# A hybrid decoder layer on one core: value projection of two head pairs in one product of 256 columns

## The chip, the core and the metric

The kernel runs on one NeuronCore of a Trainium2 chip. Its engines are TensorE (PE in the profile; PEld is its weight load), VectorE (DVE), ScalarE (ACT), GpSimd (POOL) and SyncE (SP). POOL, SP and ACT also issue DMAs, each in the order of its own instruction list. The metric is the device time of one execution in microseconds, the median of three runs. The traces come from one further execution under the hardware profiler.

## What is computed

One decoder layer on 2048 tokens of width 1024, in float32. A pre-normalised input `h` goes through one combined projection; eight heads of causal attention with a forget gate ("FoX", branch A) and eight query heads of sliding-window attention with sinks (branch B, two key/value heads) follow; each branch output is multiplied by a SiLU gate, both are concatenated, projected, normalised and added to the residual.

```python
h = rms_norm(x, g_pre[l]) * (1.0 + scale[:, None, :]) + shift[:, None, :]
proj = h @ w_in[l]
qa, ka, va, fa, za, qb, kb, vb, zb = jnp.split(proj, split_points, axis=-1)
oa = forgetting_attention(qa.reshape(B, S, FOX_HEADS, HEAD_DIM),
                          ka.reshape(B, S, FOX_HEADS, HEAD_DIM),
                          va.reshape(B, S, FOX_HEADS, HEAD_DIM), fa + b_fgate[l])
oa = oa * jax.nn.silu(za)
...
ob = sliding_window_sink_attention(qb, kb, vb.reshape(B, S, SWA_KV_HEADS, HEAD_DIM), sinks[l])
ob = ob * jax.nn.silu(zb)
y = jnp.concatenate([oa, ob], axis=-1) @ w_out[l]
x = x + gate[:, None, :] * rms_norm(y, g_post[l])
```

The change is about `va`, the values of branch A: 2048 tokens by 8 heads of 64.

## The kernel before

*Numbers.* Every float32 operand of a projection is split into a high and a low float16 part, and a product is made of three: high x high, low x high and high x low. `hT[ci]` holds the normalised input of 512 tokens (chunk `ci`, four of them), transposed: 128 features on the partitions, 8 groups of features (`k`), 512 tokens. The weights come in keys of 128 columns: `kb`, `vb`, `qb0` to `qb3` and `zb0` to `zb3` for branch B; `va0` to `va3`, `qk0` to `qk7` and `za0` to `za3` for branch A. `va0` is the value weight of heads 0 and 1, and so on in pairs of heads.

*The chain of a key's weights.* Eight steps: `w_load` (L210: one DMA of 512 KB on POOL's queue into a raw tile), `w_max` (L219: maximum per partition on DVE, then a DMA of 128 numbers to DRAM, `mx_d`, on POOL), `w_back` (L227: a DMA that reads the 128 numbers back to every partition, `mxr`, on POOL), `w_scale` (L232: a power of two from them, five small DVE instructions), `w_high` (L250: the high part, one ACT instruction), `w_low` twice (L258: the low part, two DVE instructions), `w_done` (L292: small constants). The raw tiles of all keys rotate through two buffers; the split tiles "whl" of the `va`, `zb` and `za` keys through two others.

*The products.* `proj_units` (L323) gives a projection with the weights stationary: eight units of three products of 512 columns. `value_units` (L339) keeps the tokens stationary, because attention needs the values with tokens on the partitions: for a key and a chunk eight units of 12 products of 128 columns, which fill one PSUM bank with four tiles of 128 tokens by 128 columns. After the last unit ACT copies the bank as float16 to the high half of `vt`, DVE writes the low half in two instructions, and the bank is free again. Three banks, `bk`, serve all projections of this part; `bank(True)` takes one and `release` gives it back. The inner lines:

```python
for k in range(4 * (n_ % 2), 4 * (n_ % 2) + 4):
    for n, (a, b) in enumerate(((0, 0), (1, 0), (0, 1))):
        PE.matmul(ps[:, u * P:(u + 1) * P], hT[ci][:, a, k, u * P:(u + 1) * P], whl[:, b, k, :],
                  start=(k == 0 and n == 0), stop=(k == KT - 1 and n == 2))
```

*The order.* It is written out by hand. `add` (L938) appends units to one list, `punits`, and puts the eight steps of a key's weights as events at positions ahead of its first unit: the load 42 positions ahead, the maximum 31, the read-back 21, the scale 12, the high part 9, the low parts 7 and 5, the constants 4. `fill` (L1081) walks through the list: at each position it issues the events and then the unit. A position is called a slice below. The other work is put around it with lags: `after(n, f)` runs `f` at the n-th `tick` from now.

The first 140 slices are the prologue and run alone, with a tick every second slice. Then come 32 windows of branch B (`Pair`, L852; loop at L1117). In each of them the scores (`pss`, PE), their maxima (DVE, L883), the exponentials (ACT, L894), the transposes (`pxb`, PE), the split of the transposed probabilities (`ptb`: high half on ACT, low half on DVE, L908) and the product with the values (`pob`, PE, L922) are spread over some seven or eight slices, and POOL copies the sinks (L881). The evacuation of a `zb` projection is a tanh on ACT (L376), a multiplication on DVE (L372, tile `tz`) and a DMA to DRAM on POOL (`z_d`). After the windows branch A follows, with more projections between its steps, and the output projection, whose weights and scratch go through a pool of four buffers of 2 KB per partition, `stpo` (L1375).

The projections that follow `kb`, `vb` and `zb0` stand in this order: `zb0`, `zb1`, `va0`, `zb2`, `zb3`, `va1`, `va2` in `others` (L960), mixed with `qb0` to `qb3`; then `va3` for chunks 0 and 1, `qk0`, and `va3` for chunks 2 and 3. The first unit of `va0` is slice 200; `va3` begins at slice 440.

Of the kernel before, what the change touches and what calls it, by code (L numbers as in the profile page):

```python
# [10 lines left out]
F32 = mybir.dt.float32  # L11
F16 = mybir.dt.float16
# [29 lines left out]
def hybrid_layer(  # L42
# [207 lines left out]
    def w_high(key):  # L250
        raw, pw, sw = wq[key]
        width = VB if key == "vb" else P
        pool = vbw if key == "vb" else wpq if key[0] in "qk" else wpool
        whl = pool.tile([P, 2, KT, width], F16, tag="whl", name=f"wh_{key}")
        A.activation(whl[:, 0], raw[:], AF.Identity, scale=sw[:])
        wq[key].append(whl)

# [13 lines left out]
    def o_store(on, pool, ci, rows_, cols_, eng, lag):  # L271
# [11 lines left out]
        after(lag, lambda: A.activation(oh[:, :, 0], on, AF.Copy))  # L283
        after(lag + 1, low)

    pws = {}
    scl, isc, czs, kaps = {}, {}, {}, {}

# [47 lines left out]

        return [lambda k=k: unit(k) for k in range(KT)]

    def value_units(key, ci, dst):  # L339

        st_ = {}

        def unit(n_):
            if n_ == 0:
                st_[0] = bank(True)
            whl, ps = wq[key], bk[st_[0]][:]
            u = n_ // 2
            for k in range(4 * (n_ % 2), 4 * (n_ % 2) + 4):
                for n, (a, b) in enumerate(((0, 0), (1, 0), (0, 1))):
                    PE.matmul(ps[:, u * P:(u + 1) * P], hT[ci][:, a, k, u * P:(u + 1) * P], whl[:, b, k, :],  # L350
                              start=(k == 0 and n == 0), stop=(k == KT - 1 and n == 2))
            if n_ == 7:
                hi, lo = dst()
                pv4 = ps.rearrange("p (t h d) -> p t h d", t=4, h=2)
                after(1, lambda: A.activation(hi, pv4, AF.Copy, scale=PS_SCALE))

                def low():
                    for h in range(2):
                        V.scalar_tensor_tensor(lo[:, :, h], pv4[:, :, h], PS_SCALE, hi[:, :, h],
                                               op0=ALU.mult, op1=ALU.subtract)  # L360
                    release(st_[0])

                after(2, low)

        return [lambda n=n: unit(n) for n in range(8)]

    def evac_z(kt, key, ci):
        def evac(ps, free):
# [304 lines left out]
    def open_fox():  # L673
        nonlocal abp
        xlx.close()
        abp = swa_pool("abp", 4)
        early.close()
        fxv = right.enter_context(tc.tile_pool(name="fxv", bufs=1, side="right", reuse_waits="tile"))
        vt = fx["vt"] = fxv.tile([P, NB, 8, VW], F16, name="vt")
        fx["lk"] = fxv.tile([P, LW], F16, name="lk")  # L680
# [14 lines left out]
    def va_units(j, ci):  # L695
        rows_ = slice(4 * ci, 4 * ci + 4)
        heads = slice(2 * j, 2 * j + 2)
        return value_units(f"va{j}", ci, lambda: (fx["vt"][:, rows_, heads, 0:64], fx["vt"][:, rows_, heads, 65:VW]))


    swa = ExitStack()

# [257 lines left out]
    for kind, j in (("zb", 0), ("zb", 1), ("va", 0), ("zb", 2), ("zb", 3), ("va", 1), ("va", 2)):  # L960
        key = f"{kind}{j}"
        others += [(key, va_units(j, ci) if kind == "va" else proj_units(key, ci, evac_z(4 + j, key, ci)))
                   for ci in range(NCH)]

    def at_slice(n, f):
        events.setdefault(n, []).append(f)
# [54 lines left out]
        n_o = lim  # L1021
    N_SWA = len(punits)
    at_slice(N_SWA - 40, const_turn)
    for ci in range(2):
        add("va3", va_units(3, ci))

    def evac_qk(hd, ci):
        cols_ = slice(ci * CH, (ci + 1) * CH)
# [26 lines left out]
    for ci in range(NCH):  # L1055
        add("qk0", qk_units(0, ci))
    N_QK0 = len(punits)
    for ci in range(2, NCH):
        add("va3", va_units(3, ci))
    N_V3 = len(punits)  # L1060
    for hd in range(1, 7):
        for part in range(6):
# [306 lines left out]
    def open_out():  # L1369
        nonlocal op_, stp  # L1370
        foxl.close()
        hpx.close()
        wo = foxo.enter_context(tc.tile_pool(name="wo", bufs=1, reuse_waits="tile"))
        op_ = foxo.enter_context(tc.tile_pool(name="opo", bufs=2, reuse_waits="tile"))
        stp = foxo.enter_context(tc.tile_pool(name="stpo", bufs=4, reuse_waits="tile"))  # L1375
        oio["w"] = wo.tile([P, 2, KT, D], F16, name="wohl")

        fm = sm(1, "w_p2")
        V.tensor_reduce(fm[:], fac8[:], axis=AX.X, op=ALU.max)
        V.reciprocal(fm[:], fm[:])  # L1380
        V.tensor_tensor(ysc[:], wrt[:], fm[:], op=ALU.mult)
        V.tensor_scalar(wsc[:], fac8[:], ysc[:], None, op0=ALU.mult)
# [19 lines left out]
        V.scalar_tensor_tensor(w_slot(8 + k)[:, cc], raw[:], wsc[:, k:k + 1], hi, op0=ALU.mult, op1=ALU.subtract)  # L1402

    oio = {}

    class Out:

# [315 lines left out]
```

## Time and profile before

| what | value |
|---|---|
| median of three runs | 1190.55 us (1188.28 to 1191.04) |
| the profiled execution | 1184.12 us, its span 1182.4 us |
| granted TensorE clock | 0.993 on average |
| value products (L350) | 1536 products of 128 columns, PE busy 91.0 us |
| their evacuation | 16 on ACT, 596 ns each; 32 on DVE, 416 ns each |
| a load of value weights | 4, landing 5.2 us after issue |

How to read the lines below: the page gives busy time, share of the span and count per engine, then groups of instructions as "line engine operation out<-in xcount | busy us, mean ns of one | idle time before them and what ended it". Matmuls are pipelined and their ends are modelled, so that the busy time or the mean of a product isn't what it costs; the distance from start to start is. The chain of waits follows the work that ended last backwards, and its pieces are lengths from start to start. In the timelines a bracket holds the idle time of the engine just before the instruction, and whom it waited for.

### The profile page before, as it was taken

Reading aid. Unit: us, or ns where it says so; the run is one execution under the profiler, and the core shown is the slowest. Engines: PE = TensorE matmul, PEld = TensorE weight load, DVE = VectorE, ACT = ScalarE, POOL = GpSimd, SP = SyncE. Lnnn points to the kernel's source line nnn. Section 1 sums busy time; section 2 is a strip of 40 time slices with the busy share of each in tenths; the row PEclk is TensorE's granted clock in tenths of the full one; section 3 lists DMA queues with packets and bytes.
Section 4 is the critical chain, followed back from the end, with each engine's and each line's share of the span. In section 5 each row is a group of like instructions: output and inputs, shape, how many; then the busy total and the mean of one; then the engine's idle time right before and its main releaser. Section 6 shows DMA issues by size and latency. Waiting matters only on the chain.

```text
span 1182.4 us, 27200 instructions
## 1 busy us (share of the span) xinstructions
PE 1136.7 (96%) x10757; PEld 682.6 (58%) x10757; DVE 941.3 (80%) x2311; ACT 680.9 (58%) x1150; POOL 116.1 (10%) x231
## 2 busy tenths in 40 slices
PE   5899999999999999999999999999999999999997
PEld 2476556765557986455555555555555555544444
DVE  7876678687876757688998989888898797778885
ACT  2784446565654531376766766676676788643332
POOL 2000111213122210101000100001000000000000
PEclk9899999999999999999999999999999999999999
DMA  9745433314324314333324323213211237587742
GB/s 331 263 136 88 82 93 73 87 53 109 91 63 101 54 25 90 45 85 95 66 71 57 80 66 85 60 40 77 42 42 47 58 82 242 131 212 201 197 142 107
DMA packets 123484, 120.22 MB, mean 102 GB/s; under 512 B 64948, under 2 KB 100828, under 8 KB 123356
## 3 DMA queue, kind: packets, MB, share of 16 engines
q1 hardware_dynamic: 112088, 85.69, 26.6%
q0 software_dynamic: 10832, 32.50, 13.5%
q8 instruction: 84, 1.38, 0.6%
q14 instruction: 44, 0.36, 0.1%
q10 hardware_dynamic: 436, 0.28, 0.1%
HBM read 64.75 MB, written 25.18 MB: 76 GB/s over the span
## 4 chain that ended last, share of the span: by engine, by line
PE 80%; DVE 10%; DMA 5%; issue 2%; ACT 2%; SPq 1%; DVEq 0%; ACTq 0%
PE bk L332 31%; PE bk L1520 13%; PE bk L350 7%; PE sta L1309 4%; PE sta L1308 4%; PE bk L1259 4%; PE poa L1334 3%; PE poa L1335 3%; PE poa L1332 3%; DMA wa<-in_w_ada_dram 2%; PE pxb L903 2%; PE pss L870 2%; PE pob L922 2%; DVE a_m L1262 1%; DVE pha L1322 1%
## 5 line engine op out<-in xcount | busy, mean ns | idle before, releaser
L1315 ACT ACTIVATE p<-sta,lift,scl_qk 128x1024 f32<-128x1024 f32 (+2 forms) x160 | 172.0, 1075 | 134.7 <-PE sta L1309 83.9
L332 PE MATMUL bk<-hT,wh_qk 128*128 128x512 f16 x768 | 194.0, 378 | 0.0
L1262 DVE TENSOR_REDUCE a_m<-bk 128x1 f32<-128x512 f32 x192 | 130.1, 685 | 50.2 <-PE bk L1259 49.2
L1322 DVE TENSOR_TENSOR pha<-p,pha 128x1024 f16<-128x1024 f32 (+2 forms) x160 | 169.0, 1056 | 0.2 <-ACT pha L1319 0.2
L1520 PE MATMUL bk<-wohl,oz 128*128 128x512 f16 x744 | 165.3, 379 | 1.0 <-DVE oz L1469 0.7
L1319 ACT ACTIVATE pha<-p 128x1024 f16<-128x1024 f32 (+2 forms) x160 | 148.1, 926 | 5.8 <-PE poa L1335 1.2
L1520 PEld LDWEIGHTS <-oz 128*128 128x128 f16 x744 | 71.9, 99 | 82.8 <-DVE oz L1469 1.8
L1335 PE MATMUL poa<-vt,pha 128*128 128x65 f16 x1088 | 116.1, 192 | 1.4 <-DVE pha L1322 1.2
L1332 PE MATMUL poa<-vt,pha 128*128 128x65 f16 x1088 | 116.6, 193 | 0.8 <-DVE ona L1341 0.7
L332 PEld LDWEIGHTS <-wh_qk 128*128 128x128 f16 x768 | 72.2, 97 | 77.2 <-issue 4.8
L1334 PE MATMUL poa<-vt,pha 128*128 128x64 f16 x1088 | 116.6, 194 | 0.0
L1308 PE MATMUL sta<-T 128*128 128x512 f16 (+1 forms) x320 | 110.9, 346 | 2.8 <-ACT p L1315 2.8
L1259 PE MATMUL bk<-T 66*128 66x512 f16 (+2 forms) x320 | 109.7, 348 | 3.7 <-DVE a_m L1262 2.9
L1332 PEld LDWEIGHTS <-pha 128*128 128x128 f16 x1088 | 101.5, 96 | 15.5 <-DVE ona L1341 1.8
L1309 PE MATMUL sta<-T 69*128 69x512 f16 (+1 forms) x320 | 109.8, 348 | 0.0
L1334 PEld LDWEIGHTS <-pha 128*128 128x128 f16 x1088 | 100.9, 97 | 11.4
L1335 PEld LDWEIGHTS <-pha 128*128 128x128 f16 x1088 | 100.8, 99 | 1.8 <-DVE pha L1322 1.7
L332 PE MATMUL bk<-hT,wh_za 128*128 128x512 f16 x384 | 99.7, 378 | 0.0
L350 PE MATMUL bk<-wh_va,hT 128*128 128x128 f16 x1536 | 91.0, 219 | 2.6 <-issue 2.6
L350 PEld LDWEIGHTS <-hT 128*128 128x128 f16 x1536 | 87.6, 98 | 7.6 <-issue 5.0
L332 PE MATMUL bk<-hT,wh_zb 128*128 128x512 f16 x384 | 88.9, 379 | 0.0
L332 PE MATMUL bk<-hT,wh_qb 128*128 128x512 f16 x384 | 87.4, 379 | 0.0
(505 smaller groups left out, 1890.3 us busy)
## 6 DMA issues: line engine op xcount, KB each, us to landing
hT<-in_x_dram SPq DMA_DIRECT2D x20, 512.0 KB
wa<-in_w_ada_dram SPq DMA_DIRECT2D x16, 512.0 KB
z_d<-tz POOLq DMA_DIRECT2D x32, 256.0 KB, 2.9
T<-stq SPq DMA_DIRECT2D x64, 128.0 KB
T<-z_d SPq DMA_DIRECT2D x16, 512.0 KB
out_dram<-hT SPq DMA_DIRECT2D x15, 512.0 KB
xt<-in_x_dram SPq DMA_DIRECT2D x12, 512.0 KB
qs<-qf SPq DMA_DIRECT2D x80, 64.0 KB
```

What stands on the lines that cost most here:

```text
L332: PE.matmul(ps, whl[:, a, k, :], hT[ci][:, b, k, :], start=(k == 0 and n == 0), stop=(k == KT - 1 and n == 2))
L350: PE.matmul(ps[:, u * P:(u + 1) * P], hT[ci][:, a, k, u * P:(u + 1) * P], whl[:, b, k, :], start=(k == 0 and n == 0), stop=(k == KT - 1 an ...
L1259: PE.matmul(mx[:, :w], T[0:XM, 0, i * P:(i + 1) * P], T[0:XM, 2, pc * CH:pc * CH + w], start=True, stop=True)
L1308: PE.matmul(self.st[:, o:o + w], T[:, 3, kb_], T[:, 1, qc], start=True, stop=False)
L1309: PE.matmul(self.st[:, o:o + w], T[0:XR, 2, kb_], T[0:XR, 0, qc], start=False, stop=not diag)
L1315: A.activation(self.p32[:, :self.w], self.st[:, :self.w], AF.Exp, scale=scl[f"qk{self.hd}"][:], bias=lift[:])
L1319: A.activation(self.ph[:, 0, :self.w], self.p32[:, :self.w], AF.Copy)
L1322: V.tensor_tensor(self.ph[:, 1, :self.w], self.p32[:, :self.w], self.ph[:, 0, :self.w], op=ALU.subtract)
L1332: PE.matmul(po[:, u, :], ph[:, 0, pq], vt[:, b, hd, 0:65], start=(self.first and n == 0 and u == 0), stop=False)
L1334: PE.matmul(po[:, u, 0:64], ph[:, 0, pq], vt[:, b, hd, 65:VW], start=False, stop=False)
L1335: PE.matmul(po[:, u, :], ph[:, 1, pq], vt[:, b, hd, 0:65], start=False, stop=(self.last and n == len(self.blocks) - 1))
L1520: PE.matmul(py, self.hl[:, i, k, :], w_slot(8 * j + k)[:, cc], start=(k == 0 and m_ == 0), stop=(k == KT - 1 and m_ == 2))
```

## The change

Two keys of value weights are put side by side into one tile, `wv[p]`, of 256 columns: `va0` and `va1` for p = 0, `va2` and `va3` for p = 1. One buffer holds first the one, then the other. `w_high` and `w_low` write a key's half of it. `value_units` takes a pair p and a chunk; it has 16 units of six products of 256 columns, and a bank holds two tiles of 128 tokens by four heads. The evacuation has the same instructions, over other shapes.

```diff
+        if key[:2] == "va":
+            j = int(key[2:])
+            if j % 2 == 0:
+                wv[j // 2] = fx["wv"].tile([P, 2, KT, 2 * P], F16, tag="whl", name=f"wh_va{j}")
+            whl = wv[j // 2][:, :, :, (j % 2) * P:(j % 2 + 1) * P]
+        else:
+            whl = pool.tile([P, 2, KT, width], F16, tag="whl", name=f"wh_{key}")
...
-    def value_units(key, ci, dst):
+    def value_units(p, ci, vt):
...
+            u, m = n_ // 4, n_ // 8
+            if n_ % 8 == 0:
+                st_[m] = bank(True)
+            ps = bk[st_[m]][:]
+            for k in range(2 * (n_ % 4), 2 * (n_ % 4) + 2):
                 for n, (a, b) in enumerate(((0, 0), (1, 0), (0, 1))):
+                    PE.matmul(ps[:, (u % 2) * 2 * P:(u % 2 + 1) * 2 * P], hT[ci][:, a, k, u * P:(u + 1) * P],
+                              wv[p][:, b, k, :], start=(k == 0 and n == 0), stop=(k == KT - 1 and n == 2))
+            if n_ % 8 == 7:
+                t0, heads = 4 * ci + 2 * m, slice(4 * p, 4 * p + 4)
+                hi, lo = vt[:, t0:t0 + 2, heads, 0:64], vt[:, t0:t0 + 2, heads, 65:VW]
+                pv4 = ps.rearrange("p (t h d) -> p t h d", t=2, h=4)
```

The units of a pair and a chunk go into the list in two halves of eight. The order of the projections becomes `zb0`, `zb1`, `va01`, `zb2`, `zb3`, `va23`, so that all of `va1` comes before `zb2`; `va23` for chunk 2 stands after the windows' last units and for chunk 3 after `qk0`. In `add`, each of the two keys keeps its own eight steps, and those of the first key of a pair are put 48 slices further ahead:

```diff
-        if key not in pkeys and key not in ("kb", "vb"):
+        if key in ("va01", "va23"):
+            for j in key[2:]:
+                add(f"va{j}", [])
+        elif key not in pkeys and key not in ("kb", "vb"):
...
+                if key in ("va0", "va2"):
+                    lead += 48
...
-    for kind, j in (("zb", 0), ("zb", 1), ("va", 0), ("zb", 2), ("zb", 3), ("va", 1), ("va", 2)):
+    for kind, j in (("zb", 0), ("zb", 1), ("va", 0), ("zb", 2), ("zb", 3), ("va", 1)):
         key = f"{kind}{j}"
+        if kind == "va":
+            others += [(("va01", "va23")[j], us) for ci in range(4 - 2 * j) for us in va_units(j, ci)]
+        else:
+            others += [(key, proj_units(key, ci, evac_z(4 + j, key, ci))) for ci in range(NCH)]
```

By slices: `va01` takes its units from 200 to 303, `zb2` from 312, `zb3` from 368, `va23` from 408. The steps of `va0` are at 110 (load), 121 (maximum), 131 (read-back), 140 (scale), 143 (high), 145 and 147 (low); those of `va1` are where `va0` had them, from 158 on; those of `va2` from 318 on, its high part at 351; those of `va3` where `va2` had them, from 366 on.

The pool for `wv` takes 8 KB per partition for the rest of the kernel. The output projection's four buffers of 2 KB are taken from it: a second tile in the same buffer, handed out in quarters in rotation.

```diff
-        stp = foxo.enter_context(tc.tile_pool(name="stpo", bufs=4, reuse_waits="tile"))
+        stp = Quarters(fx["wv"].tile([P, 2, KT, 2 * P], F16, tag="whl", name="sv"))
...
+        def tile(self, shape, dtype, **kw):
+            v = self.flat[:, self.n * HALF:(self.n + 1) * HALF]
+            self.n = (self.n + 1) % 4
```

More of the change, by code (lines that the diff above doesn't have):

```diff
@@ L337, in proj_units @@
         return [lambda k=k: unit(k) for k in range(KT)]
[L339 removed]
+    def value_units(p, ci, vt):
         st_ = {}
         def unit(n_):
[L344 to L348, printed above, removed]
[L349 to L354 removed]
+            u, m = n_ // 4, n_ // 8
[3 more added lines that the diff above has]
+            for k in range(2 * (n_ % 4), 2 * (n_ % 4) + 2):
+                for n, (a, b) in enumerate(((0, 0), (1, 0), (0, 1))):
+                    PE.matmul(ps[:, (u % 2) * 2 * P:(u % 2 + 1) * 2 * P], hT[ci][:, a, k, u * P:(u + 1) * P],
[4 more added lines that the diff above has]
+                pv4 = ps.rearrange("p (t h d) -> p t h d", t=2, h=4)
                 after(1, lambda: A.activation(hi, pv4, AF.Copy, scale=PS_SCALE))
                 def low():
[L358 to L359 removed]
+                    for t in range(2):
+                        V.scalar_tensor_tensor(lo[:, t], pv4[:, t], PS_SCALE, hi[:, t],
                                                op0=ALU.mult, op1=ALU.subtract)
[L361 removed]
+                    release(st_[m])
                 after(2, low)
[L365 removed]
+        return [lambda n=n: unit(n) for n in range(16)]
     def evac_z(kt, key, ci):
@@ L679, in open_fox @@
         vt = fx["vt"] = fxv.tile([P, NB, 8, VW], F16, name="vt")
+        fx["wv"] = right.enter_context(tc.tile_pool(name="wv", bufs=1, side="right", reuse_waits="tile"))
         fx["lk"] = fxv.tile([P, LW], F16, name="lk")
@@ L693, in const_turn, with va_units, va_group @@
         after(1, lambda: A.activation(fx["crow"][64:XR, :], px[64:XR, 0:P], AF.Copy))
[L695 to L698, printed above, removed]
+    def va_units(p, ci):
+        us = [lambda n=n: va_group(p, ci)[n]() for n in range(16)]
+        return us[:8], us[8:]
+    va_made = {}
+    def va_group(p, ci):
+        if (p, ci) not in va_made:
+            va_made[p, ci] = value_units(p, ci, fx["vt"])
+        return va_made[p, ci]
     swa = ExitStack()
@@ L1023, in hybrid_layer @@
     at_slice(N_SWA - 40, const_turn)
-    for ci in range(2):
-        add("va3", va_units(3, ci))
+    for us in va_units(1, 2):
+        add("va23", us)
     def evac_qk(hd, ci):
@@ L1057, in hybrid_layer @@
     N_QK0 = len(punits)
-    for ci in range(2, NCH):
-        add("va3", va_units(3, ci))
+    for us in va_units(1, 3):
+        add("va23", us)
     N_V3 = len(punits)
@@ L1404, in hybrid_layer, with __init__ @@
     oio = {}
+    class Quarters:
+        def __init__(self, whole):
+            self.flat, self.n = whole[:].rearrange("p a k n -> p (a k n)"), 0
+        def tile(self, shape, dtype, **kw):
+            v = self.flat[:, self.n * HALF:(self.n + 1) * HALF]
+            self.n = (self.n + 1) % 4
+            if dtype == F32:
+                return v.bitcast(F32)
+            if dtype == BF16:
+                v = v.bitcast(BF16)
+            return v.rearrange("p (a b) -> p a b", a=shape[1])
     class Out:
```

4 lines of the change are left out of this document (1 added, 3 removed).

## The prediction

> **What bounds the kernel now.** I read the page first, then the table by stage, the chain of waits, and last the engines' timelines between 120 and 185 us, where the change moves work.
>
> ```profile
> span 1182.4 us, 27200 instructions
> PE 1136.7 (96%) x10757; PEld 682.6 (58%) x10757; DVE 941.3 (80%) x2311; ACT 680.9 (58%) x1150; POOL 116.1 (10%) x231
> ...
> L350 PE MATMUL bk<-wh_va,hT 128*128 128x128 f16 x1536 | 91.0, 219 | 2.6 <-issue 2.6
> L350 PEld LDWEIGHTS <-hT 128*128 128x128 f16 x1536 | 87.6, 98 | 7.6 <-issue 5.0
> ```
>
> PE (TensorE) is busy for 96% of the span, and the group that the change rewrites is its 1536 value products at L350. A share over the whole span decides nothing, so the stage comes next (stretch, length, then busy time and instructions of PE, weight loads, DVE, ACT and POOL):
>
> ```profile
> 130.00:435.00 305.00, 302.18 (x3393) 206.18 (x3391) 224.90 (x647) 165.60 (x450) 61.77 (x140) 1.00 0.33 75
> 169.00:184.00 15.00, 14.75 (x126) 8.31 (x125) 14.53 (x45) 8.42 (x23) 2.17 (x5) 1.00 0.38 90
> ```
>
> Most of the value products run between 202 and 435 us. From 130 to 435 us PE is busy for 302.2 of 305 us at full granted clock (1.00) and DVE for only 224.9, so a microsecond of PE saved there shortens the kernel by a microsecond. The second stretch is the exception: from 169 to 184 us DVE is busy for 14.5 of 15 us. The chain of waits (start, length, what; the factor counts instructions) gives the price of a product by width, because its lengths run from start to start:
>
> ```profile
> 375.80 1.44 issue
> ...
> 407.79 1.12 issue
> ...
> 424.94 10.72 PE bk L350 x192
> 439.77 10.38 PE bk L332 x48
> ...
> 1169.32 5.25 PE bk L1484 x48
> ```
>
> A product of 128 columns takes 10.72/192 = 55.8 ns, one of 512 takes 10.38/48 = 216.3 ns, one of 256 takes 5.25/48 = 109.4 ns (the last output tile, L1484). All three lie on 0.417 ns a column plus 2.5 ns a product: the weight loads are hidden already at 128 columns.
>
> **The change part by part.**
>
> *Products.* 1536 x 55.8 = 85.8 us become 768 x 109.4 = 84.0 us: 1.8 us less, on PE's path, with nothing to hide it. Bounds: 768 fixed shares of 2.5 ns are 1.9 us, so 1.7 to 2.0.
>
> [...]
>
> *Issue gaps.* Twice, at 375.80 and 407.79 us, PE stops inside L350 for nothing that the profile shows, 2.56 us together. Both lie where value products follow each other almost without a break, at two instructions per 55.8 ns; among products of 512 columns (two per 216 ns) PE has no such gap. Halving the instructions should remove them. Bounds: nothing to 2.6 us; I take 2.6, since the new pace (two per 109 ns) lies nearer to the side without gaps.
>
> [...] The trace does not show what the two gaps wait for.
>
> *Evacuation.* Two heads of four tiles become four heads of two tiles: per bank still one ACT copy of 512 columns and two DVE instructions of 256, so many banks as before. Zero; if they were slower, DVE's free quarter would cover it.
>
> *Order of products.* zb2 and zb3 change places with the value products. Units have the same length (12 x 55.8 = 670 ns, now 6 x 109.4 = 656 ns), the same three banks serve them, and the weight chains of zb2, qb3, zb3 and va3 keep the spacing that other keys had at these slices. Zero. The single tile "wv" makes va2's ACT split wait for the last product of va01; that is slice 303 against 351, a wait long over.
>
> *Tail.* The four staging buffers become quarters of one tile. Each load still waits for the last reader of its own quarter, and the list of waits is as long as before. Zero.
>
> *The early value weights.* Here is the cost. va0's chain moves 48 slices ahead: load at slice 110, maximum 121, read-back 131, scale 140. In the prologue a slice lasts 0.65 us, and these are the landing times (count, KB, median us from issue):
>
> ```profile
> mxr<-mx_d POOLq DMA_DIRECT2D x23, 64.0 KB, 5.0
> ...
> mx_d<-w_mx POOLq DMA_DIRECT2D x23, 0.5 KB, 8.0
> ```
>
> The fastest and the slowest of mxr's 23 landings, from the view of that tile:
>
> ```profile
> DMA to landing us min/median/max: 3.9/5.0/6.7
> ```
>
> POOL issues these transfers in order, and the read-back waits on POOL until the maximum has landed:
>
> ```profile
> 123.10 0.55 POOL L224 DMA_DIRECT2D mx_d<-w_mx  x1 [11.68 <-DVE w_mx L221]
> ...
> 131.04 0.54 POOL L229 DMA_DIRECT2D mxr<-mx_d  x1 [4.77 <-DMA mx_d<-w_mx]
> 145.13 0.54 POOL L374 DMA_DIRECT2D z_d<-tz  x1 [13.55 <-DVE tz L372]
> 145.67 0.91 POOL L215 DMA_DIRECT2D wr_qb<-in_w_in_dram  x1
> 146.57 0.53 POOL L881 COPY sm__1811<-snk 128x2 f32<-128x2 f32 x2
> ...
> 155.81 0.54 POOL L224 DMA_DIRECT2D mx_d<-w_mx  x1 [0.57 <-DVE w_mx L221]
> ...
> 165.11 0.54 POOL L229 DMA_DIRECT2D mxr<-mx_d  x1 [6.53 <-DMA mx_d<-w_mx]
> ```
>
> Between the two it took 7.9 us once and 9.3 us once. The instructions of DVE around which va0's steps are put:
>
> ```profile
> 139.03 0.28 DVE L240 TENSOR_REDUCE w_mx<-mxr 128x1 f32<-128x128 f32 x1
> ...
> 139.99 0.68 DVE L733 SCALAR_TENSOR_TENSOR qc<-bk,cosT 128x512 f32<-128x512 f32 x1
> 141.11 0.29 DVE L810 SCALAR_TENSOR_TENSOR nf<-nf,na 128x128 f32<-128x128 f32 x1 [0.44 <-ACT na L807]
> 142.15 0.75 DVE L261 SCALAR_TENSOR_TENSOR wh_zb<-wr_zb,w_sw,wh_zb 128x512 f16<-128x512 f32 x1 [0.75 <-ACT wh_zb L255]
> ...
> 150.97 0.17 DVE L887 TENSOR_SCALAR b_nb<-b_m 128x4 f32<-128x4 f32 x1
> 153.70 0.69 DVE L372 SCALAR_TENSOR_TENSOR tz<-tz,bk 128x512 f32<-128x512 f32 x1 [2.56 <-ACT tz L376]
> 154.31 1.21 DVE L221 TENSOR_REDUCE w_mx<-wr_qb 128x1 f32<-128x1024 f32 x1
> ...
> 157.54 0.69 DVE L737 TENSOR_TENSOR stb<-qc,stb 128x512 f16<-128x512 f32 x1 [0.70 <-ACT stb L747]
> 159.03 0.54 DVE L883 CUSTOM_DVE_ANT_0 sm__1909<-pss,bmask,snk 128x256 f32<-128x256 f32 x1 [0.80 <-PE pss L870]
> ...
> 161.70 0.95 DVE L908 TENSOR_TENSOR ptb<-pxb,ptb 128x768 f16<-128x768 f32 x1
> ```
>
> In the changed order va0's maximum stands just before 139.99. Its raw weights, issued at about 131.6 behind the read-back, land some 5 us later, so it starts at once; its 1.1 us disappear in the idle 0.44 + 0.75 that follow. Its mx_d then leaves at 139.99 + 1.1 + 0.3 = 141.4, lands at 149.4, and the mxr behind it lands at 154.4. va0's scale (five small instructions, 0.96 us by 139.03 to 139.99) stands behind b_nb and before tz: DVE stops at 151.1 and goes on at 154.4, scale done at 155.4. Queued behind it are tz and all that follows. On ACT, va0's split (1.14 us) waits for the scale and stands before the tanh:
>
> ```profile
> L261 DVE SCALAR_TENSOR_TENSOR wh_va<-wr_va,w_sw,wh_va x8: 721/746/748, 197.1 to 421.6; 128x512 f16<-128x512 f32 x8
> ...
> L255 ACT ACTIVATE wh_va<-wr_va,w_sw x4: 1133/1140/1149, 193.8 to 416.7; 128x1024 f16<-128x1024 f32 x4
> ...
> 153.00 0.67 ACT L376 ACTIVATE tz<-bk,cz_zb 128x512 f32<-128x512 f32 x1
> ...
> 164.65 0.69 PE L922 MATMUL pob<-vb,ptb 128*128 128x64 f16 x18
> ...
> 182.65 0.81 PE L922 MATMUL pob<-vb,ptb 128*128 128x64 f16 x22 [0.25 <-DVE ptb L908]
> ```
>
> The split ends at 156.5, the tanh at 157.2, and DVE's tz starts at 157.2 instead of 153.70. From tz to the lower half of ptb DVE took 161.70 - 153.70 = 8.0 us; now two lower halves of va0 and its kappa are added (1.5 us) and the idle 0.70 + 0.80 goes. ptb is ready at 157.2 + 8.0 + 0.95 = 166.1 us. PE asks for it in its pv at 164.65 + 0.1: it waits 1.4 us, in a stage that gives nothing back. Bounds: mxr at its fastest, 3.9, leaves 0.3; 9.3 and mxr's slowest, 6.7, instead of 8.0 and 5.0 make it 3.0 more, 4.4 us. A gain is excluded, since the step only adds work.
>
> The same queue then delays qb1. Its load leaves at about 150 instead of 145.67, its maximum 3 us later, its read-back lands at about 172 (158.8 + 8.0 + 5.0), where DVE wants it at 172.5 (171.1 before, plus the 1.4). Free, or up to 2.3 us with 9.3 and 6.7; I take 0.3. It matters because DVE is full there, and PE waits for it at 182.65 already. What POOL's copies of snk feed (ACT's exponentials at 151.2) is late by 0.2 us at most.
>
> *Sum.* -1.8 - 2.6 + 1.4 + 0.3 = -2.7 us. The profiled execution took 1184.1 us (span 1182.4 and 1.7 around it) and would take 1181.4. The median of the runs lies 6.4 us above it; the same difference from 1190.55 gives **1187.9 us**.
>
> **The rivals.**
>
> 1. *The early chain costs nothing* (landings nearer the fastest): -4.4, 1186.2. For it: DVE was idle for 2.56 us at just this place. Against: two landings in series need 13 us, and the slices allow 12.
> 2. *The gaps stay.* They belong to a transfer of instructions that comes late anyway: -1.8 + 1.7, 1190.5. For it: there were only two in 1536 products.
> 3. *Slower: the wait for va0's scale repeats.* Place: DVE behind POOL's read-backs, at va0 (151 us) and again at qb1 (172 us). Price: 4.4 + 2.3 = 6.7 us by the slow landings; with the gaps kept, 1190.55 - 1.8 + 6.7 = 1195.5. It decides once the two waits together exceed 4.4 us, or 1.8 if the gaps stay. For it: DVE is full from 169 to 184. Against: it needs landings slower than the median, twice.
> 4. *Weight loads bind at 128 columns* after all: PEld shows 87.6 us for 1536 loads, 57.0 ns each; if the 768 dropped ones came out whole, 43.8 us, 1146.8. Against: the 2.5 ns per product that three widths share. [...]
>
> That the change does not do what it says is excluded: PE's list is shorter by 768 products and 768 loads, and the value products have 256 columns.
>
> **How the numbers follow.** Forecast 0.37, rival 1 0.25, rival 2 0.12, rival 3 0.24, rival 4 0.02. A measurement of this kernel tells about 0.3%, 3.6 us, from no change: faster is below 1187.0, slower above 1194.1. Faster: rival 1, rival 4 and 0.03 of the forecast, 0.30. Slower: 0.20 of rival 3. Same: 0.50. The forecast's own range is 1186 to 1190; the range over the cases, from a little under rival 1 with the runs' spread of 2.8 us to rival 3, is 1183 to 1195.
>
> **What would show it.** In the profile after: 768 products of about 84.0 us; no "issue" row inside them; DVE idle for about 3 us before L240 at 151 us with the DMA of mxr as releaser; PE idle for 1 to 2 us before pv at 165 us. The prediction is wrong if PE shows idle time above 3 us in 150 to 185 us, new idle time after 200 us, or a 256-column product off 109 ns by more than 2.

## The result, and the profile after

| | changed | before |
|---|---|---|
| median | 1195.69 us (1192.61 to 1199.13, 6 runs) | 1188.98 us (1187.86 to 1191.04, 6 runs) |
| profiled execution, span | 1194.16 us, 1192.5 us | 1184.12 us, 1182.4 us |
| granted TensorE clock | 0.989 | 0.993 |

The ratio of the times is 1.0054, with a 95% interval of 1.0037 to 1.0070: 0.5% slower. (The six runs of the kernel before are the three of the first table and three more.) The two profiled spans lie 10.0 us apart, the medians 6.7: the profiled execution of the kernel before is a fast one, 3.7 us below the lowest of its six runs. Executions of one kernel spread over 2 to 8 us and chips differ (the medians of the kernel before run from 1184 to 1193 us below), so times are compared on one chip only.

Where do the 10.0 us lie? The end is not it. These are the first scores of branch A, in the PE timelines of before and after:

```profile
481.68 0.38 PE L1308 MATMUL sta<-T 128*128 128x512 f16 x1
```

```profile
491.72 0.38 PE L1329 MATMUL sta<-T 128*128 128x512 f16 x1
```

They are 10.04 us apart, as the ends are; what follows costs the same. The first value product starts at 202.45 us before and 207.91 after: 5.46 us are gone by then. From there to the last value product it is 271.7 us before and 274.5 after, 2.7 more in spite of fewer products, and from there to the row above 7.5 and 9.35, 1.8 more. Each of the three has its place; the third isn't the change's.

**The first stop.** PE at the first scores of the windows, before and after (start, length, what, idle time before it and what ended that):

```profile
145.57 2.75 PE L332 MATMUL bk<-hT,wh_zb 128*128 128x512 f16 x12
148.26 0.68 PE L870 MATMUL pss<-kst,stb 64*128 64x128 f16 x12
```

```profile
145.50 2.75 PE L339 MATMUL bk<-hT,wh_zb 128*128 128x512 f16 x12
151.56 0.29 PE L884 MATMUL pss<-kst,stb 64*128 64x128 f16 x4 [3.31 <-ACT stb L761]
152.28 0.56 PE L884 MATMUL pss<-kst,stb 64*128 64x128 f16 x8 [0.44 <-DVE stb L751]
152.77 4.45 PE L339 MATMUL bk<-hT,wh_zb 128*128 128x512 f16 x12
```

`stb` is late because DVE waits for `qs`, the queries' halves that SP exchanges by DMA for the rotary embedding. DVE and POOL of the changed kernel:

```profile
149.42 0.69 DVE L757 TENSOR_TENSOR qs<-qs,sinT 128x512 f32<-128x512 f32 x1 [3.65 <-DMA qs<-qf]
```

```profile
141.76 0.56 POOL L224 DMA_DIRECT2D mx_d<-w_mx  x1 [9.21 <-DVE w_mx L221]
```

Before, the same DVE instruction ran at 145.52 us without a wait. The four `qs` transfers leave SP at about the same time in both (141.5 and 141.8 us on), and their last data packet has moved by 145.4 us in both. Late is the landing. The trace has 16 landing times for each of these transfers; in the changed kernel, sorted, they are:

```
store mx_d      143.45 143.91 144.24 145.40 146.66 ... 148.39 148.40 148.47
first qs        143.63 144.08 144.42 145.57 146.81 ... 148.54 148.56 148.68
fourth qs       145.47 145.51 145.53 146.09 147.37 ... 149.00 149.06 149.30
```

The first `qs` lands 0.15 to 0.21 us behind the store of va0's maximum, one by one: the store, 128 pieces of 4 bytes to DRAM, lands up to 6.7 us after its issue, and by this pairing what came behind it lands no earlier. Before, the 16 times lie from 143.25 to 143.47 us for the first `qs` and from 145.18 to 145.40 for the fourth. Why one landing follows the other, the trace, which names no DMA engine for them, doesn't show; that such a store alone makes `qs` late is the result of *before_mxd* below.

The stop costs a second time, in the windows table (stretch, length, busy time and count of PE, PEld, DVE, ACT, POOL, then the granted clock):

```profile
152.00:156.00 4.00, 3.72 (x17) 1.48 (x18) 3.34 (x15) 0.68 (x3) 0.00 (x0) 0.63 0.79 206
156.00:160.00 4.00, 4.00 (x19) 1.77 (x18) 1.32 (x3) 2.80 (x8) 0.17 (x1) 0.94 0.10 30
```

After 3.75 us of idle time the granted clock is at half for 3.41 us, from 153.07 us: the 12 products from 152.77 take 4.29 us to the next one's start, where 12 x 216.3 ns are 2.60. So 3.31 + 0.44 + 1.7 = 5.4 us, the whole of the first part.

**The second stop.** PE, ACT, POOL and DVE of the changed kernel at 341 to 353 us:

```profile
342.11 2.98 PE L339 MATMUL bk<-hT,wh_zb 128*128 128x512 f16 x13
346.64 3.18 PE L339 MATMUL bk<-hT,wh_zb 128*128 128x512 f16 x14 [1.55 <-issue]
...
353.26 0.81 PE L936 MATMUL pob<-vb,ptb 128*128 128x64 f16 x22 [3.38 <-DVE ptb L922]
```

```profile
346.78 1.02 ACT L926 ACTIVATE ptb<-pxb 128x1024 f16<-128x1024 f32 x1 [5.89 <-remote]
```

```profile
346.84 0.30 POOL L895 COPY sm__4599<-snk 128x2 f32<-128x2 f32 x2 [6.12 <-remote]
```

```profile
346.95 0.54 DVE L897 CUSTOM_DVE_ANT_0 sm__4599<-pss,bmask,snk 128x256 f32<-128x256 f32 x1 [5.30 <-remote]
...
351.02 0.29 DVE L240 TENSOR_REDUCE w_mx<-mxr 128x1 f32<-128x128 f32 x1 [1.92 <-DMA mxr<-mx_d]
```

Three engines are released within 0.2 us at 346.8, by what the profile calls "remote"; what they wait for is PE's scores and transposes, which ended at 342.2. Some 4.5 us lie between the two. Meanwhile 15 of the 4 KB packets on POOL's queue take 2.3 to 9.6 us (their median from 336 to 352 us is 0.16), and PE itself stops for 1.55 us, for nothing that the profile shows. Then DVE is late with the maxima, waits for the read-back of va2's maximum (issued at 337.68 us, landed 13.3 us later), and PE waits 3.38 us for `ptb`; half a clock follows. 1.55 + 3.38 + 1.7 = 6.6 us, against which stand the gains of the products (1.8) and of the two gaps (2.6): 2.2 of the 2.7.

**The third part** is the clock alone. DVE's maxima of the keys stop PE twice near 485 us (before, near 477 us, 1.26 and 1.57 us), and of these two traces only the later one has the clock fall behind them:

```profile
484.89 0.22 PE L1280 MATMUL bk<-T 66*128 66x128 f16 x1 [1.38 <-DVE a_m L1283]
...
487.33 0.22 PE L1237 MATMUL bk<-identh,lq 128*72 128x128 f16 x1 [1.58 <-DVE a_m L1283]
```

```profile
488.00:491.00 3.00, 3.00 (x8) 1.06 (x7) 2.44 (x9) 0.00 (x0) 0.00 (x0) 0.50 0.00 1
```

The change isn't the cause: of the runs below, *before_row*, with the old order and the narrow products, has the half clock here too (from 474.24 us), while *both* and *row_va0*, with the wide products, have the two waits and no half clock.

**The clock.** All three stretches at half clock in this part of the changed kernel's trace last 3.41 us. They begin at 153.07, 354.45 and 487.57 us, 201.38 and 133.12 us apart, which is 59 and 39 times 3.413; one in the prologue begins at 101.87 us, 15 times 3.413 ahead of the first. In this trace they lie on a fixed grid. The same length of that grid just ahead of each, and one without a half clock behind it, in the changed kernel:

```profile
149.66:153.07 3.41, 1.07 (x14) 0.56 (x15) 2.75 (x6) 1.11 (x2) 1.22 (x3) 1.00 0.54 47
351.04:354.45 3.41, 1.19 (x27) 1.19 (x28) 3.27 (x10) 2.36 (x6) 0.56 (x1) 1.00 0.59 166
484.16:487.57 3.41, 1.11 (x6) 0.51 (x6) 3.24 (x11) 0.00 (x0) 0.03 (x1) 1.00 0.59 147
344.22:347.63 3.41, 1.86 (x10) 0.78 (x8) 0.68 (x3) 0.85 (x1) 0.30 (x2) 1.00 0.64 13
```

PE was busy for 1.07 to 1.19 of 3.41 us ahead of the three halvings. After the 1.86 us of the last row there was none, nor in the kernel before after 1.83 us (476.74 to 480.15 us). In these traces the halving goes with how much of one such length a stop empties, not with how long it is: 2.39 and 0.44 us of waiting fall into one length in *rowpair* (0.86 us busy) and halve the clock, 3.06 us fall across two in *both* (1.61 and 2.17 us busy) and don't. From 1.2 to 1.9 us both outcomes occur: the clock halves after 1.34 us in the kernel before, at 101.27 us, after 1.61 in *va2_24*, at 125.08, and after 1.86 in the changed kernel, at 101.87; in *before_mxd* it doesn't after 1.52, at 394.64.

**The products** are as predicted. 48 of them take 213.15 - 207.91 = 5.24 us, 109.2 ns each, and their group has no idle time:

```profile
207.91 5.40 PE L357 MATMUL bk<-wh_va,hT 128*128 128x256 f16 x48
213.15 0.54 PE L936 MATMUL pob<-vb,ptb 128*128 128x64 f16 x13
```

```profile
L357 PE MATMUL bk<-wh_va,hT 128*128 128x256 f16 x768 | 89.1, 273 | 0.0
```

### The profile page after: what moved, and what is told of

Same layout as the page of the kernel before. It is cut to its first block, busy times and chain, and to the rows that moved or that the text cites. A ratio compares the mean times of both kernels' runs of the same rounds, so it can differ in the third digit from the quotient of the medians.

```text
span 1192.5 us, 25661 instructions
## 1 busy us (share of the span) xinstructions
PE 1139.4 (96%) x9989; PEld 673.4 (56%) x9989; DVE 941.2 (79%) x2311; ACT 680.1 (57%) x1150; POOL 115.7 (10%) x231
## 3 DMA queue, kind: packets, MB, share of 16 engines
q0 software_dynamic: 10832, 32.50, 13.7%
## 5 line engine op out<-in xcount | busy, mean ns | idle before, releaser
L357 PE MATMUL bk<-wh_va,hT 128*128 128x256 f16 x768 | 89.1, 273 | 0.0
L357 PEld LDWEIGHTS <-hT 128*128 128x128 f16 x768 | 74.3, 98 | 13.3 <-issue 1.9
```

The source lines that it names most:

```text
L357: PE.matmul(ps[:, (u % 2) * 2 * P:(u % 2 + 1) * 2 * P], hT[ci][:, a, k, u * P:(u + 1) * P], wv[p][:, b, k, :], start=(k == 0 and n == 0), ...
```

## The experiments

Theory: the small stores to DRAM, moved to new places, hold back other transfers; the products themselves are worth what was predicted. Rivals: the 512 KB load, the order on POOL, the wide products, or chance. Ratios are to the kernel before, on the same chip.

**again** (no edit), **before_mxd** (the store alone, in the kernel before), **lead40** and **zb2first** (va0's chain elsewhere) ran on one chip.

> The changed kernel once more, for a second trace of it. Theory (the small store of va0's maximum holds back the landings of the qs transfers queued behind it): pss at about 148 us waits again for stb, 2 to 4 us, and qs lands 3 to 4 us after the last of its data; the first value product starts near 207 us. Rival (a chance event of that one execution): no wait above 0.5 us there, first value product near 202.5 us. The stop of all engines at 342 to 347 us is expected not to be there again (no instruction of the change is near it); if it is at the same place, the change causes it.

Measured: 1197.18 us, ratio 1.0045 (1.0026 to 1.0064). PE waits 3.7 us at `pss`, DVE 5.0 us for `qs`, and the stop of all engines is there too (gap 2.1 us, wait for `ptb` 3.9). Both stops belong to the kernel; that the second wouldn't return was wrong.

```diff
+    def extra():
+        mx = sm(1, "w_mx")
+        V.tensor_reduce(mx[:], wq["zb1"][0][:], axis=AX.XY, op=ALU.max, apply_absolute_value=True)
+        G.dma_start(mx_d[3][:], mx[:])
...
+    at_slice(121, extra)
```

> The kernel before with one more maximum (of zb1's raw weights, its result unused) and its 0.5 KB store at slice 121, where the changed kernel has va0's; no load, no read-back, no scale. Theory (the store holds the landings of qs): DVE waits for qs about 3 to 4 us from 146 us on, PE idle 2 to 4 us at pss, 3 to 5.5 us slower in the span. Rival (va0's 512 KB load, or the read-backs in POOL's order, cost the time): the first value product stays within 1 us of 202.5 and the span within 1.2 us (the maximum itself).

Measured: 1199.10 us, 1.0055 (1.0036 to 1.0074), as slow as the changed kernel. DVE, then PE:

```profile
151.25 0.69 DVE L743 TENSOR_TENSOR qs<-qs,sinT 128x512 f32<-128x512 f32 x1 [5.38 <-DMA qs<-qf]
```

```profile
153.38 0.40 PE L870 MATMUL pss<-kst,stb 64*128 64x128 f16 x4 [4.62 <-ACT stb L747]
```

A store of 0.5 KB that nobody reads makes the first stop, without the load and the read-back; for this stop these rivals are out. The loss is larger than expected, since PE waits another 5.0 us for `ptb` in five places.

```diff
-                    lead += 48
+                    lead += 40 if key == "va0" else 48
```

> The changed kernel with va0's chain 40 instead of 48 slices ahead: its store leaves after the four qs transfers. Theory: no wait for qs at 146 us, PE idle below 0.5 us at pss, first value product 4 to 5.5 us earlier than in the changed kernel (202.5 to 204 us); time 4 to 5.5 us below the changed kernel's. Rival (the load's traffic costs it): the load comes 5 us later and meets qs itself, so the wait stays, 2 to 4 us. Rival (the read-back stalls DVE, as predicted): idle before L240 of 3 us and a wait of 1 to 3 us at pv.

Measured: 1195.19 us, 1.0021 (1.0003 to 1.0039), 2.0 below *again*, half of the least that was expected. The wait at `pss` is gone; but PE waits 1.98 us at 169 us and 1.06 at 188 for `ptb`, and the second stop is unchanged (2.3 and 3.3 us). POOL tells why: the read-back waits for the store, and the copy of the sinks is queued behind it, on which ACT's exponentials wait.

```profile
155.65 0.55 POOL L229 DMA_DIRECT2D mxr<-mx_d  x1 [6.45 <-DMA mx_d<-w_mx]
156.19 0.31 POOL L895 COPY sm__1821<-snk 128x2 f32<-128x2 f32 x2
```

```diff
-    for kind, j in (("zb", 0), ("zb", 1), ("va", 0), ("zb", 2), ("zb", 3), ("va", 1)):
+    for kind, j in (("zb", 0), ("zb", 1), ("zb", 2), ("va", 0), ("zb", 3), ("va", 1)):
...
-                    lead += 48
+                    lead += 40 if key == "va0" else 48
```

> The changed kernel with zb2 ahead of the first two value heads instead of behind them, and va0's chain 40 slices ahead of them: all of va0's chain lies after 185 us, none in the prologue. Theory: prologue as in the kernel before (pss without a wait, 202.5 us reached with the same work), so the gains of the products (1.8 us) and of the gaps (2.6 us) stand alone: 4 us below the kernel before, 9 to 10 below the changed one. Rival (the wide products or their evacuation cost time themselves): not faster than the kernel before.

Measured: 1203.21 us, 1.0084 (1.0054 to 1.0113): the slowest, where 4 us below the kernel before were expected. The first scores don't wait, as expected, but the read-backs are late elsewhere, and PE waits 4.0, 4.4 and 5.3 us for `ptb`. Two of DVE's waits:

```profile
244.30 0.29 DVE L240 TENSOR_REDUCE w_mx<-mxr 128x1 f32<-128x128 f32 x1 [3.96 <-DMA mxr<-mx_d]
...
353.98 0.29 DVE L240 TENSOR_REDUCE w_mx<-mxr 128x1 f32<-128x128 f32 x1 [6.71 <-DMA mxr<-mx_d]
```

The rival's time came, not its cause: what PE waits for is `ptb`, 13.7 us in these three places, and *row2* below settles what the products cost. Moving a chain moves the trouble. So the next runs took the store's target away, or spread the chains.

**row**: no maximum goes to DRAM.

```diff
-        md = mx_d[len(kaps_seen) % 3]
...
-        G.dma_start(md[:], mx[:])
...
+        mxr = mxp.tile([P, P], F32, tag="mxr", name="mxr")
+        G.dma_start(mxr[0:1, :], mx[:])
...
-        G.dma_start(mxr[:], wq[key].pop().rearrange("p o -> (p o)").partition_broadcast(P))
+        G.dma_start(mxr[1:P, :], mxr[0:1, :].unsqueeze(1).broadcast_to([1, P - 1, P]))
```

> The changed kernel, its order untouched; every maximum goes as a row of 128 numbers into partition 0 of the tile mxr in SBUF instead of to DRAM, and the read-back copies that row to the other 127 partitions. Theory (a store of 128 pieces of 4 bytes to DRAM is acknowledged late, 6 to 8 us, and holds back the landings of other transfers on the same DMA engines): the row lands in 2 to 4 us, the wait at pss at about 150 us is below 1 us, the stop of all engines at 341 to 347 us is gone or below 1.5 us; 5 to 9 us below the changed kernel. Rival (it is the order on POOL, or the traffic of the load): both waits stay, within 2 us of the changed kernel. A partial result (one wait gone) says that the two have different causes.

Measured: 1176.47 us, 0.9874 (0.9846 to 0.9902): 14.7 us below the kernel before. The changed kernel didn't run on this chip; with its ratios elsewhere (1.0045 to 1.0054) *row* is some 20 us below it, more than twice what was expected. Neither stop is left, and no gap. The issues' table (KB, median us to landing), after the change and in *row*:

```profile
mx_d<-w_mx POOLq DMA_DIRECT2D x23, 0.5 KB, 8.3
```

```profile
mxr<-w_mx POOLq DMA_DIRECT2D x23, 0.5 KB, 2.0
```

The same 128 pieces of 4 bytes, issued by the same queue, land in 2.0 us in SBUF and in 8.3 us in DRAM.

**va2_24** moves va2's chain away from zb3's; **split** keeps va0's load early but puts store and read-back behind `qs` and the sinks; **both** does both.

```diff
-                if key in ("va0", "va2"):
-                    lead += 48
+                if key == "va0":
+                    lead += (48, 40, 36, 36)[min(n, 3)]
+                if key == "va2":
+                    lead += 24
```

This is *both*; *va2_24* keeps 48 for all of va0's steps, *split* keeps 48 for va2.

> The changed kernel with va2's chain 24 instead of 48 slices ahead: zb3's store and read-back no longer lie 4 us behind va2's. Theory for the second stop (two stores and a read-back close together, with z_d and o_d behind them): the wait for ptb at 353 us (3.4 to 3.9 us) and the gap of 1.6 to 2.3 us ahead of it are gone, 4 to 6 us below the changed kernel, the wait at pss stays. Rival (the stop hangs on the place in the program, not on these transfers): both stay where they are.

> The changed kernel with va0's load where it is, its maximum 8 slices later, its read-back 12 and its scale 12 slices later: the store leaves behind the qs transfers and the read-back behind the copies of snk on POOL. Theory (landings held by the store; in lead40 the rest was the read-back ahead of the copies of snk): no PE wait above 0.5 us from 145 to 200 us, 4 to 5.5 us below the changed kernel. Rival (two chains are too much for the prologue whatever their order): PE waits of 2 us or more stay at pss or pv.

> split and va2_24 together. If the two stops are the whole loss and independent: 8 to 11 us below the changed kernel, 2 to 4 us below the kernel before (the gains of products, 1.8 us, and of gaps, 2.6 us, are left). If the products themselves bring nothing: equal to the kernel before within 1.5 us.

Measured: *va2_24* 1190.44 us, 0.9987 (0.9970 to 1.0005). The second stop is gone, the first stays (3.31 and 0.44 us): as expected. *split* 1196.13 us, 1.0036 (1.0021 to 1.0051): no wait at `pss`, but PE waits 2.20 us at 170 us and 1.06 at 189, and the second stop stays; less than expected; in its trace qb1's load lands late now (DVE waits 3.9 us for it). *both* 1187.09 us, 0.9958 (0.9941 to 0.9976), 4.0 below the kernel before although 3.06 us of waiting remain at 170 us and 1.06 at 189. Each stop can be had without the other, and order alone is enough to make the change pay.

**before_row** is the control: the kernel before with *row*'s edit. **row_stores** puts two stores back into *row*.

> The kernel before (128-column products, its own order of weight chains) with the maxima as rows in SBUF, as in row. It is the control for row: what row gained may have little to do with the change. Theory A (the stores to DRAM cost the kernel before 6 to 10 us too, the two gaps of 2.6 us in the value products among them, and without them the wide products are worth only their 1.8 us): 1178 to 1182 us, row 1 to 4 us below it. Theory B (the gaps belong to the 128-column products' rate of instructions): the two gaps of 1.1 to 1.4 us inside L350 are still there and row is 4 us or more below. Theory C (the wide products bring nothing): equal to row within 1 us.

> row once more, on the chip of before_row, for a comparison of the two: 1174 to 1179 us if the earlier figure holds.

```diff
+        if key in ("va2", "zb3"):
+            G.dma_start(mx_d[key == "zb3"][:], mx[:])
```

> row with two stores of 0.5 KB to DRAM put back, beside the rows: the maxima of va2 and zb3, stored as the changed kernel stores them, read by nobody. Theory (the stores alone make the second stop, whoever reads them): all engines stop for 2 to 5 us some 6 to 12 us behind the second store (near 320 to 335 us), and the span grows by 2 to 6 us over row. Rival (it takes the read-back from DRAM as well): no stop, span within 1.5 us of row's.

Measured, on one chip: *before_row* 1181.05 us, 0.9917 (0.9902 to 0.9931); *row2* 1176.45, 0.9885 (0.9868 to 0.9903); *row_stores* 1177.72, 0.9885 (0.9863 to 0.9906). Theory A: the stores cost the kernel before 9.0 us already, and without them the change is worth 4.6 us by the medians, a little more than the 1 to 4 of the theory (by the ratios and their intervals, 1 to 6.5). The products explain 2.0 of it, and the two profiled spans are only 1.8 us apart; the rest isn't assigned. Of the 9.0 us the two traces, with spans of 1182.4 and 1179.6 us, show 2.8: the gaps, and a wait ahead of all value products (DVE waits 5.95 us for `sinT`, a rotary table, at 117.46 us in the kernel before and not in *before_row*). The groups of the value products in *before_row* and *row2*:

```profile
L348 PE MATMUL bk<-wh_va,hT 128*128 128x128 f16 x1536 | 90.7, 219 | 0.0
```

```profile
L355 PE MATMUL bk<-wh_va,hT 128*128 128x256 f16 x768 | 89.1, 273 | 0.0
```

1536 narrow products, and no gap: theory B falls, and with 4.6 us so does C. Summed from start to start, the products take 85.96 us in *before_row* and 83.97 in *row2*, 1.99 less. In *row_stores* there is no stop, with both stores taking 9.3 us to land: these two stores alone don't make the second one.

**row_back** and **row_read** looked for what does.

```diff
+        if key in ("va2", "zb3"):
+            G.dma_start(mx_d[("va2", "zb3").index(key)][:], mx[:])
+        else:
+            G.dma_start(mxr[0:1, :], mx[:])
...
+        if key in ("va2", "zb3"):
+            G.dma_start(mxr[:], mx_d[("va2", "zb3").index(key)].rearrange("p o -> (p o)").partition_broadcast(P))
+            return
```

```diff
+        if key == "qb0":
+            G.dma_start(mx_d[0][:], mx[:])
...
+        if key in ("va2", "zb3"):
+            spare = mxp.tile([P, P], F32, tag="mxr", name="mxr")
+            G.dma_start(spare[:], mx_d[0].rearrange("p o -> (p o)").partition_broadcast(P))
```

> row with the whole way through DRAM put back for va2 and zb3 alone (store, POOL's wait for it, read-back to 128 partitions); the other maxima stay rows in SBUF. Theory (the second stop comes from a read-back from DRAM beside stores that are still under way; row_stores had the stores alone and no stop): all engines stop for 2 to 5 us near 330 to 345 us, PE waits 3 to 4 us for ptb behind it, half the clock for 3.4 us, 4 to 8 us above row. Rival (the stop needs the state that many such stores leave): no stop, within 1.5 us of row.

> row with two read-backs from DRAM to 128 partitions that nobody uses, issued beside those of va2 and zb3; what they read was stored at slice 67, some 200 us earlier. If reading one 512 B line of DRAM 128 times is what stops the engines: a stop of 2 to 5 us near 325 to 345 us, also here. If it takes a store under way: no stop, and the span within 1.5 us of row's.

Measured: 1177.69 us, 0.9874 (0.9849 to 0.9899), and 1181.98 us, 0.9909 (0.9878 to 0.9939). No second stop in either. *row_read* is 4.3 us slower than *row_back*, and not by its read-backs at 331 and 339 us: its first value product is already 4.4 us later (204.50 against 200.14 us). What differs ahead of that is the one store to DRAM of qb0's maximum, issued at 102.55 us and landed 9.2 us later. Behind it SP's loads of the rotary tables are late, and DVE waits:

```profile
118.50 0.69 DVE L760 TENSOR_TENSOR qs<-qs,sinT 128x512 f32<-128x512 f32 x1 [8.02 <-DMA cosT<-cs__242]
```

In *row_back* the same instruction runs at 110.64 us without a wait. PE then waits 0.93 and 0.87 us for `hT`, and the clock is at half for 3.41 us from 123.91 us. So a single store of 0.5 KB, in a kernel that sends nothing else of this kind to DRAM by then, holds up the prologue as va0's does in the changed kernel.

**rowpair** and **row_va0** are the counterparts: the changed kernel with only va2's and zb3's, or only va0's, maximum as a row (the edit of *rowpair*; the other has `("va0",)`).

```diff
+        if key in ("va2", "zb3"):
+            mxr = mxp.tile([P, P], F32, tag="mxr", name="mxr")
+            G.dma_start(mxr[0:1, :], mx[:])
...
+        if key in ("va2", "zb3"):
+            mxr = wq[key][-1]
+            G.dma_start(mxr[1:P, :], mxr[0:1, :].unsqueeze(1).broadcast_to([1, P - 1, P]))
```

> The changed kernel with va2's and zb3's maxima alone as rows in SBUF, the other 21 by DRAM: the counterpart of row_back. If these two stores and read-backs take part in the second stop: no gap and no wait for ptb at 341 to 354 us, 4 to 7 us below the changed kernel; the first stop at pss stays, 3 to 4 us. If the stop hangs on what the other stores leave behind: it stays, within 1.5 us of the changed kernel.

> The changed kernel with va0's maximum alone as a row in SBUF. Theory for the first stop (this one store holds the landings of qs): no wait at pss, first value product 4 to 5.5 us earlier, the second stop stays; 4 to 5.5 us below the changed kernel.

Measured: *rowpair* 1184.37 us, 1.0000 (0.9985 to 1.0016), the second stop gone, the first there (2.39 and 0.44 us). *row_va0* 1179.19 us, 0.9958 (0.9942 to 0.9975): both stops gone, though va2 and zb3 still go by DRAM and the second was expected to stay. This chip was faster (1183.79 for the kernel before), so *row_va0* and the changed kernel were run together:

> The changed kernel a third time, on the chip of row_va0b, because row_va0 was free of both stops on a chip on which every kernel ran some 6 us faster. If the second stop hangs on the chip or its state: here it is there or not as in row_va0b. If it follows from the first (the program reaches the place 7 us later): here both stops, in row_va0b neither, 9 to 12 us apart.

> row_va0 once more, beside again2. If the second stop is a matter of how the transfers fall in time: no stop, 9 to 12 us below again2. If it was the chip: the second stop as in the changed kernel, 4 to 5.5 us below again2, the price of the first stop alone.

Measured: *again2* 1190.51 us, 1.0049 (1.0034 to 1.0063); *row_va0b* 1180.51, 0.9965 (0.9952 to 0.9979). They are 10.0 us apart, and it was not the chip, which is as fast (1184.28 for the kernel before): *again2* has a first stop of 0.78 and 0.44 us and the second one (wait for `ptb` 3.2 us), *row_va0b* neither.

## Why the prediction was wrong

Predicted were 1187.9 us, no change most likely; it came out at 1195.69. Step by step:

*Products:* right. 109.2 ns each for 109.4; from start to start 1.99 us less in *row2* than in *before_row*, for 1.8.

*Issue gaps:* they left the value products, as predicted, but the reason given, the rate of instructions, is wrong: *before_row* has all 1536 products and no gap, and the changed kernel has one of 1.55 us among products of 512 columns. The gaps go when the maxima no longer pass through DRAM. Rival 2, that they belong to a transfer of instructions that comes late anyway, was nearer in one of the two. The DMA view names packets of kind "instruction"; 84 of 16 KB on queue q8 in the kernel before and 78 in the changed one, for 21514 and 19978 instructions of PE and PEld, are one for every 256. Between 394.3 and 406.2 us the kernel before moves none of them, where *before_row* moves one at 398.9; the next takes from 406.27 to 407.32 us, and PE stops at 407.79. What held it up isn't shown. The gap at 375.80 us and the changed kernel's at 345 us have no packet that starts late.

*The early value weights:* this is the step that failed. The store of va0's maximum was priced as a delay of its own reader alone (8.0 us to land, then 5.0). That what lands behind it comes late too (the last landing of `qs` at 149.30 us for 145.40) was not in the sum, and SP's queue, which it is moved past, was not looked at: four `qs` transfers leave in the same 3 us, and their reader, the first scores, had no slack. That cost 3.31 and 0.44 us of waiting and 1.7 us of half clock, where +1.7 us were allowed for the whole step. What the step did price came out harmless, hidden by the first stop. The scale, the product with the values and qb1's scale in the changed kernel, without a bracket:

```profile
155.13 0.28 DVE L240 TENSOR_REDUCE w_mx<-mxr 128x1 f32<-128x128 f32 x1
...
176.67 0.26 DVE L240 TENSOR_REDUCE w_mx<-mxr 128x1 f32<-128x128 f32 x1
```

```profile
170.24 0.69 PE L936 MATMUL pob<-vb,ptb 128*128 128x64 f16 x18
```

mxr was issued at 149.01, for 149.4 predicted; the chain's own times were right. Where the first stop is taken away by order alone (*split*), a wait at that product does appear, 2.20 us, but with qb1's load as the late one.

*Order of products:* "zero" was wrong as well. The text checked the chains of zb2, qb3, zb3 and va3 and not va2's, which is moved to within 4 us of zb3's. *va2_24* undoes that, and with it goes the second stop, 6.6 us by the changed kernel's trace.

*The clock:* behind each of the two stops 3.41 us at half clock cost 1.7 us again, which no term held; the third (1.11 us busy ahead of it, 1.83 before and no half clock) is put down to the chance of where the grid lies.

*Rival 3*, slower, named 1195.5 us, near the result, but by waits of DVE for read-backs at 151 and 172 us; neither is in the trace. The number is a coincidence. *Rival 1*, 4.4 us for a chain that costs nothing, is near what the change is worth once the store is out of the way: 4.6 and 3.8 us in *row_va0* and *row_va0b* against the kernel before, 4.6 in *row2* against *before_row*. In the last pair there are no gaps to win, so the agreement there is in the number only.

What stays open is the second stop. Taking any one of va0's store, va2's and zb3's stores, or va2's place away removes it; a store, a read-back or both, put into a kernel that has none, don't bring it. All kernels with it have stores to DRAM under way; which coincidence sets it off was not found.

## What to carry to other kernels

When a step is moved, list the transfers that are in flight on every queue at its new place, and ask for each whose landing has no slack; here a store of 0.5 KB was enough for 3.31 us of waiting. Passing a maximum per partition through a row in SBUF instead of DRAM was worth 9.0 us in the kernel before and some 20 in the changed one (*row*, the fastest version found, is 14.7 us below the kernel before). And a stop of TensorE can cost 1.7 us more than its length, by 3.41 us at a granted clock of 0.50: in these traces that followed where it left TensorE, at full clock, busy for 0.86 to 1.19 us of one 3.41 us length of the clock's grid, and in some cases where 1.3 to 1.9 us were left. An edit that moves the work in time moves it against that grid, so a difference of 1.7 us between two single traces may be nothing but that.

## What was not expected of the hardware

- 128 pieces of 4 bytes land in 2.0 us in SBUF (*row*) and in 8.0 (the kernel before) to 8.3 us (the changed one) in DRAM, from the same queue: four times as long.
- In the changed kernel DVE, ACT and POOL start at 346.8 us on what PE ended at 342.2, some 4.5 us later, while PE goes on for 3 us; the profile shows "issue" at PE and "remote" elsewhere.
- Two waits of 1.38 and 1.58 us, 0.9 us of work between them, are followed by half the clock in the changed kernel, and 1.26 and 1.57 us in the one before aren't: PE is busy for 1.11 of 3.41 us in one length of the clock's grid in the first, and for 1.83 or more in the one before.
